# A decoder step's MLP with a third result buffer, finishing work spread over steps, and six row operands kept in high and low parts

## The chip, the core and the metric

The kernel runs on one core of one Trainium2 chip. The metric is the device time of one execution in microseconds. The kernel before took 2792.03 us as the median of three runs (2787.6 to 2799.4). The profile is of one further execution.

The engines named below: TensorE (PE, with PEld for its weight loads), VectorE (DVE), ScalarE (ACT), GpSimd (POOL) and SyncE (SP). POOL and SP mostly issue transfers here, each on a queue of its own. Every engine works through its own instructions in the order in which the program emits them, and waits where an operand is not there yet.

## What is computed

One step of a one-layer decoder for 576 rows (512 of a prompt, 64 of eight samples), all in float32. Cut to what matters here:

```python
D_MODEL = 2048; D_FF = 4 * D_MODEL

x = x + jnp.concatenate([attn, conv_y], axis=-1) @ w_out
hid = jnp.square(jax.nn.relu(rms_norm(x, g_mlp) @ w_up))
x = x + hid @ w_down
gate = jax.nn.sigmoid(rms_norm(x, g_ple) @ w_ple_gate)
x = x + (pe @ w_ple) * gate
y = rms_norm(x, g_final)
```

Ahead of that stand the input projections, attention over a prompt and over a paged cache, and a convolution. The change does not touch them.

## The kernel before

**Phases.** The first phase (up to 860 us of the profile) holds projections, attention and convolution. Then comes the out-projection, 16 output tiles from `outproj` (L1155), up to 1069 us. The second phase (`phase2`, L1300) is the MLP: `up` (group g=1, 32 passes), `down` (g=2, 8 output pairs over 32 operands, cut into rounds), and the gate (g=3, 8 passes), to 2756 us; a final norm and the stores follow.

**Products.** Operands lie transposed, features on the 128 partitions and rows on the free axis. `up` and `down` work on blocks of two by two (a pair of feature tiles, two halves of HR = 288 rows) with seven products instead of eight. Seven sums of weight blocks meet seven sums of row blocks. Each operand is split for TensorE's float32r form into a high part (rounded, an ACT copy) and a low part (the rest, a DVE subtraction), and a product is three matmuls: high by high, high by low, low by high. One *step* is one weight quad against one row operand: 7 products, 21 matmuls of 128 x 288, lines L1460 to L1462. Steps are numbered from 0 at the start of `up`: 256 of `up` (8 per pass), 256 of `down`, then 64 of the gate, whose products are plain.

**A pass's end.** The seven products lie in seven of eight PSUM tiles. `combine_head` (L1543) and `combine_tail` (L1557) add them into a result pair `c` of [128, 2, 576], one of two buffers. The next pass's products need these PSUM tiles: the first has the eighth, the second waits for the ACT copy L1550, the third for L1551, and so on. A pass's *finish* (`fin_up`, `fin_down`, `fin_gate`, `fin_out` for the out-projection) then makes from `c` what the next group needs. `fin_up` scales by the norm (L1314), applies relu and square (L1316, L1317), makes the row sums `T` (`tsums`, L1513) and stores them with `c` to DRAM (`stored`, L1277) as seven blocks in float32, 1008 KB for an operand.

**Row operands.** A ring of eight places holds row operands with high and low parts, [128, 2, 7, 288] each. When a place's last use is past, a hook calls `mk` (L1364): it loads the next stored operand, 1008 KB, into the low half (L1376, on POOL's queue) and queues a *build* (`slot`, L1534): two ACT copies make the high part, two DVE subtractions (864 and 1152 columns) turn the loaded sums into the low part. For the first `up` pass operands 0, 1 and 7 are made in place by `fin_out`, 2 to 6 are loaded once the first phase's operands are off TensorE. At the last `up` pass, steps 248 to 255, the eight places change to `down`'s operands 0 to 7, one per step. `down`'s first round is short: passes of 3, 3, 3, 4, 5, 6, 7 and 8 steps.

**Weights.** `QStream` (L1620) loads two quads at a time on SP's queue (512 KB into one of four `w2r` buffers), sums blocks on DVE (L1648 to L1650) and splits one quad per step into `w2h` (ACT) and `w2l` (DVE), three buffers each, two steps ahead (`prep(t + 2)`).

**Order.** The program writes out each engine's order by hand. `Beside` (L1574) holds two queues of generators, 0 for finishes and 1 for builds. Within each step `run` gives the step's time as credit (2.79 us) and takes pieces from queue 0 first, then 1, while credit lasts. A piece yields its DVE cost; a negative yield -k makes its generator rest for k steps. `EL` (L95) estimates the costs. `flush` emits a generator to its end at once, as when a step needs an operand whose build is not out yet, or at a pass's end, where queue 0 is emptied. The finish of the last `up` pass goes to queue 1.

```python
self.credit = min(max(self.credit, -3.0) + dt, dt)
while self.credit > 0:
    ready = [q[0] for q in self.q if q and q[0][1] <= t]
```

Of the kernel before, what the change touches and what calls it, by code (L numbers as in the profile page):

```python
# [30 lines left out]
DOWN_PART = 7  # L31
RING = 8
OUT_ORDER = (0, 1, 4, 5, 6, 7, 2, 3)

# [108 lines left out]
class Kern:  # L143
# [52 lines left out]
    def build(self):  # L196
        tc, nc, a = self.tc, self.nc, self.a
        with ExitStack() as top:
# [956 lines left out]
    def outproj(self, gen):  # L1155

        nc, a = self.nc, self.a
        self.open2()
        bg, t2 = self.bg, self.t2
        for n in range(KT):  # L1160
            self.on = n
            if n % 2 == 0:
                bg.flush_all(0)
                self.oc_ = t2.tile([128, 2, NR], F32, name="c", tag="c", bufs=2)
            self.rx = t2.tile([128, NR], F32, name="rx", tag="rx", bufs=1)
            nc.sync.dma_start(self.rx, a["x"][:, n, :])
# [12 lines left out]
            gen = self.gemm_tile(self.out_evac)  # L1179
# [36 lines left out]
    def plan(self):  # L1216
# [9 lines left out]
        wsrc = (None, a["w_up"], a["w_down"], a["w_gate"])  # L1226
        loads = []
        for g, p, k0, k1 in segs:
            for k in range(k0, k1, 2):
                m = min(2, k1 - k)  # L1230
                loads.append((wsrc[g][p][:, k:k + m], m, g == 3))
        self.segs = segs
        self.W = QStream(self, loads, EL)
# [10 lines left out]
    def squares(self, p, x):  # L1244

        nc, acc = self.nc, self.acc2
        sq = self.buf("sq2")
        nc.scalar.activation(sq, x, AF.Square)
        yield 0
        if p == 0:  # L1250
            nc.vector.tensor_tensor(acc, sq[:, 0, :], sq[:, 1, :], ALU.add)
            yield EL(NR)
        else:
            for i in range(2):
                nc.vector.tensor_tensor(acc, acc, sq[:, i, :], ALU.add)
                yield EL(NR)
# [8 lines left out]
    def operands(self, c, g):  # L1265

        if g is not None:
# [3 lines left out]
            c = cg  # L1271
            yield 0
# [4 lines left out]
    def stored(self, c, T, dst):  # L1277
        nc = self.nc
        nc.gpsimd.dma_start(dst[:, 0, :], c[:, 0, :HR])
        nc.gpsimd.dma_start(dst[:, 1:3, :].rearrange("p a n -> p (a n)"), c[:, 1, :])  # L1280
        nc.gpsimd.dma_start(dst[:, 3:, :], T)

    def fin_out(self, p, c):
# [10 lines left out]
        else:  # L1294
            self.stored(cg, T, self.up_in[p])
        if p == 7:
            yield from self.squares(p, c)
            self.bg.add(0, self.norm(self.P_))

    def phase2(self):  # L1300
# [12 lines left out]
        def fin_up(p, c, r, final):  # L1313
# [3 lines left out]
            nc.scalar.activation(c, c, AF.Square)  # L1317
            yield 0
            c, T = yield from self.operands(c, None)
            self.stored(c, T, self.down_in[p])  # L1320

# [42 lines left out]
        def mk(g, j):  # L1364
# [9 lines left out]
            def load():  # L1374
                bg.flush(fin_of[g - 1, j])
                nc.gpsimd.dma_start(f(h.lo), src)  # L1376

            if g < 3:
                load()

            def build():
# [14 lines left out]

        quadlist = [(si, k) for si, sg in enumerate(segs) for k in range(sg[2], sg[3])]
        lastuse, seg0 = {}, {}
# [30 lines left out]
        slots[1, 7].work = fin_of[0, 7]  # L1429
        prev = before = behind = None  # L1430
        for t, (si, k) in enumerate(quadlist):
            g, p, k0, k1 = segs[si]
            if prev:
# [16 lines left out]
            hi, lo = W.hl.pop(t)  # L1450
            if k == k0:
                pr = {}
            if g == 3:
                self.plain(pr, hi, lo, s, k == k0, k == k1 - 1)
            else:
                for (i, ia, ib) in self.PRODS:
                    if k == k0:
                        pr[i] = self.P_()
                    o = pr[i][:, :HR]
                    nc.tensor.matmul(o, hi[:, ia, :], s.hi[:, ib, :], start=(k == k0), stop=False)  # L1460
                    nc.tensor.matmul(o, hi[:, ia, :], s.lo[:, ib, :], start=False, stop=False)  # L1461
                    nc.tensor.matmul(o, lo[:, ia, :], s.hi[:, ib, :], start=False, stop=(k == k1 - 1))  # L1462
# [7 lines left out]
            if g == 1 and p == 0 and 2 <= k + 2 < 7:  # L1470
                bg.flush(slots[1, k + 2].work)
            if k == k1 - 1:
                if g != 1 or p:
                    bg.flush_all(0)
                if slow:
                    r = pre[g](p, lastseg[g, p] == si)
                if before:
                    bg.flush(before)
                if g == 3:
                    c = t2.tile([128, 2, NR], F32, name="c", tag="c", bufs=2)  # L1480
                else:
# [61 lines left out]
    def combine_head(self, pr):  # L1543

        nc, t2 = self.nc, self.t2
        q = lambda i: pr[i][:, :HR]
        c = t2.tile([128, 2, NR], F32, name="c", tag="c", bufs=2)
        c11, c12, c22 = c[:, 0, :HR], c[:, 0, HR:], c[:, 1, HR:]
# [25 lines left out]
class Beside:  # L1574


    def __init__(self):
        self.q = [deque(), deque()]
        self.credit, self.now = 0.0, 0
# [21 lines left out]
    def run(self, t, dt):  # L1601
# [18 lines left out]
class QStream:  # L1620
# [15 lines left out]
    def sums(self, l):  # L1636
# [6 lines left out]
        if self.loads[l][2]:  # L1643
# [127 lines left out]
```

## Time and profile before

| | us |
|---|---|
| median of three runs | 2792.03 |
| profiled execution | 2789.04 |
| its span | 2787.3 |
| PE busy | 2702.0 (97%) |
| DVE busy | 2058.4 (74%) |
| ACT busy | 1174.4 (42%) |
| POOL busy | 503.5 (18%) |

The span runs from the first to the last instruction; the execution's time adds what lies around it. Matmuls are pipelined, so PE's busy time overstates its work: where PE lost time is read from the number of matmuls in a stretch instead. A window row gives start and end, length, busy time and instruction count (x) for each engine, the granted TensorE clock (1.00 is full), the DMA engines' busy share, and GB/s. A group or timeline row names line, engine, operation, output and input tile, and in brackets the idle time before it and what ended that. Tiles named `xs` are row operands in the ring, `c` is a result pair, `t` or `wt` a helper of the combination, `ui` and `di` the stored operands of `up` and `down`, `x` the residual in DRAM.

### The profile page before, as it was taken

Reading aid. Unit: us, or ns where it says so; the run is one execution under the profiler, and the core shown is the slowest. Engines: PE = TensorE matmul, PEld = TensorE weight load, DVE = VectorE, ACT = ScalarE, POOL = GpSimd, SP = SyncE. Lnnn points to the kernel's source line nnn. Section 1 sums busy time; section 2 is a strip of 40 time slices with the busy share of each in tenths; the row PEclk is TensorE's granted clock in tenths of the full one; section 3 lists DMA queues with packets and bytes.
Section 4 is the critical chain, followed back from the end, with each engine's and each line's share of the span. In section 5 each row is a group of like instructions: output and inputs, shape, how many; then the busy total and the mean of one; then the engine's idle time right before and its main releaser. Section 6 shows DMA issues by size and latency. Waiting matters only on the chain.

```text
span 2787.3 us, 56961 instructions
## 1 busy us (share of the span) xinstructions
PE 2702.0 (97%) x22201; PEld 2605.8 (93%) x22201; DVE 2058.4 (74%) x3613; ACT 1174.4 (42%) x1755; POOL 503.5 (18%) x896
## 2 busy tenths in 40 slices
PE   8999999999999999999999999989999999999996
PEld 8988889998888998999999999989999999999995
DVE  5677777766654437888888888898888888888444
ACT  4232334345643324444444444544444444444332
POOL 1177766731100000000000000100000000000000
PEclk9999999999999999999999999999999999999998
DMA  4688888888745445444444444655665556555444
GB/s 151 204 286 274 288 284 290 292 299 303 261 141 193 150 154 201 135 149 140 142 142 137 141 138 136 240 148 165 173 177 158 166 170 173 170 175 192 155 157 167
DMA packets 232432, 530.81 MB, mean 190 GB/s; under 512 B 25217, under 2 KB 25858, under 8 KB 232162
## 3 DMA queue, kind: packets, MB, share of 16 engines
q1 hardware_dynamic: 167234, 329.72, 36.7%
q0 software_dynamic: 32096, 137.67, 15.6%
q10 hardware_dynamic: 32832, 59.78, 6.9%
q8 instruction: 174, 2.85, 0.4%
q14 instruction: 96, 0.79, 0.1%
HBM read 431.53 MB, written 95.55 MB: 189 GB/s over the span
## 4 chain that ended last, share of the span: by engine, by line
PE 61%; issue 5%; DVE 4%; ACT 1%; DMA 1%; POOL 0%; DVEq 0%; ACTq 0%; SPq 0%; POOLq 0%
PE P L1461 15%; PE P L1460 15%; PE P L1462 15%; PE U L478 7%; PE P L1503 2%; PE P L1505 2%; PE P L1504 2%; PE U L1109 1%; DVE w2l L152 1%; DVE xs L152 1%; DMA xs<-x 0%; DMA xs<-ui 0%; DVE y L1491 0%; DVE w2r L1648 0%; DMA w2r<-in_w_up 0%
## 5 line engine op out<-in xcount | busy, mean ns | idle before, releaser
L1460 PE MATMUL P<-xs,w2h 128*128 128x288 f32 x3584 | 1066.1, 297 | 20.7 <-DVE c L1551 9.6
L1461 PE MATMUL P<-xs,w2h 128*128 128x288 f32 x3584 | 1065.3, 297 | 4.6 <-DVE xs L152 4.6
L1462 PE MATMUL P<-xs,w2l 128*128 128x288 f32 x3584 | 1061.4, 296 | 3.1 <-DVE w2l L152 3.1
L149 ACT ACTIVATE w2h<-w2r 128x896 fp32r<-128x896 f32 (+1 forms) x576 | 523.4, 915 | 772.2 <-PE P L1461 462.1
L152 DVE TENSOR_TENSOR w2l<-w2r,w2h 128x896 fp32r<-128x896 f32 (+1 forms) x576 | 600.5, 1043 | 208.0 <-ACT w2h L149 207.3
L1460 PEld LDWEIGHTS P<-xs,w2h 128*128 128x128 f32 x3584 | 678.1, 189 | 27.4 <-DVE c L1551 12.5
L1461 PEld LDWEIGHTS P<-xs,w2h 128*128 128x128 f32 x3584 | 678.6, 189 | 6.8 <-DVE xs L152 6.5
L1462 PEld LDWEIGHTS P<-xs,w2l 128*128 128x128 f32 x3584 | 676.5, 189 | 3.8 <-DVE w2l L152 3.8
L478 PE MATMUL U<-xh,whi 128*128 128x288 f32 x1792 | 401.5, 306 | 2.7 <-ACT whi L123 1.4
L478 PE MATMUL U<-xh,wlo 128*128 128x288 f32 x1792 | 385.0, 296 | 2.5 <-DVE wlo L129 2.5
L478 PE MATMUL U<-xl,whi 128*128 128x288 f32 x1792 | 383.9, 296 | 2.0 <-DVE xl L311 2.0
L478 PEld LDWEIGHTS U<-xh,whi 128*128 128x128 f32 x1792 | 288.1, 189 | 23.5 <-issue 16.9
L478 PEld LDWEIGHTS U<-xh,wlo 128*128 128x128 f32 x1792 | 288.5, 189 | 3.7 <-DVE wlo L129 3.7
L478 PEld LDWEIGHTS U<-xl,whi 128*128 128x128 f32 x1792 | 288.5, 189 | 3.2 <-DVE xl L311 3.2
L123 ACT ACTIVATE whi<-wraw 128x512 fp32r<-128x512 f32 x224 | 141.2, 630 | 284.6 <-PE U L478 153.5
L129 DVE TENSOR_TENSOR wlo<-wraw,whi 128x512 fp32r<-128x512 f32 x224 | 159.7, 713 | 102.5 <-ACT whi L123 100.3
L1019 DVE SCALAR_TENSOR_TENSOR y<-ue,cv,y 128x512 f32<-128x512 f32 x240 | 183.3, 764 | 4.2
L1648 DVE TENSOR_TENSOR w2r<-w2r 128x512 f32<-128x512 f32 (+1 forms) x272 | 177.7, 653 | 10.2 <-DMA w2r<-in_w_up 5.1
L1020 POOL TENSOR_SCALAR cvt<-us,cv 128x64 f32<-128x64 f32 x240 | 168.6, 702 | 21.8
L1503 PE MATMUL P<-xs,w2h 128*128 128x288 f32 x512 | 152.2, 297 | 0.1
L1504 PE MATMUL P<-xs,w2h 128*128 128x288 f32 x512 | 151.4, 296 | 0.0
L1505 PE MATMUL P<-xs,w2l 128*128 128x288 f32 x512 | 151.4, 296 | 0.0
(347 smaller groups left out, 2947.7 us busy)
## 6 DMA issues: line engine op xcount, KB each, us to landing
k<-in_cache_kv SPq DMA_DIRECT2D x256, 256.0 KB, 5.0
v<-in_cache_kv SPq DMA_DIRECT2D x256, 256.0 KB, 5.0
w2r<-in_w_up SPq DMA_DIRECT2D x128, 512.0 KB, 4.0
w2r<-in_w_down SPq DMA_DIRECT2D x112, 512.0 KB, 4.3
wraw<-in_w_main ACTq DMA_DIRECT2D x156, 256.0 KB, 5.1
xs<-di POOLq DMA_DIRECT2D x32, 1008.0 KB, 6.1
x<-c POOLq DMA_DIRECT2D x48, 576.0 KB, 7.3
di<-T POOLq DMA_DIRECT2D x32, 576.0 KB, 3.6
```

What stands on the lines that cost most here:

```text
L149: self.nc.scalar.activation(out, in_, AF.Copy, **kw)
L152: self.nc.vector.tensor_tensor(out, in_, f(hi), ALU.subtract)
L478: self.nc.tensor.matmul(u[:, r, :HR], w, x[:, r * HR:(r + 1) * HR], start=first and n == 0, stop=last and n == 2)
L1019: nc.vector.scalar_tensor_tensor(y, ue[:, j:j + NPR], w, y, ALU.mult, ALU.add)
L1020: nc.gpsimd.tensor_scalar(t, us[:, :, j:j + 8], w, None, ALU.mult)
L1460: nc.tensor.matmul(o, hi[:, ia, :], s.hi[:, ib, :], start=(k == k0), stop=False)
L1461: nc.tensor.matmul(o, hi[:, ia, :], s.lo[:, ib, :], start=False, stop=False)
L1462: nc.tensor.matmul(o, lo[:, ia, :], s.hi[:, ib, :], start=False, stop=(k == k1 - 1))
L1503: nc.tensor.matmul(o, hi[:, ia, :], s.hi[:, kh, rows], start=first and kh == 0, stop=False)
L1504: nc.tensor.matmul(o, hi[:, ia, :], s.lo[:, kh, rows], start=False, stop=False)
L1505: nc.tensor.matmul(o, lo[:, ia, :], s.hi[:, kh, rows], start=False, stop=last and kh == 1)
L1648: lambda: V(w[:, :, 4:6, :], w[:, :, 0:1, :].broadcast_to([128, m, 2, 128]), w[:, :, 1:3, :], ALU.add),
```

## The change

Six operands, the pairs in `SPLIT` (group, number), are stored in DRAM already split, [128, 2, 7, 288] of float32r. `stored` makes each part where the sums are: four pieces (288 columns and three of 576), each an ACT copy, a rest of one step, a DVE subtraction, two POOL transfers and another rest. For the `down` operands all four pieces use one buffer `hl`. `mk` loads such an operand whole, 2016 KB, into its place and queues no build.

Result pairs have three buffers instead of two, and a finish must be out only before its buffer is needed again, three passes later, while `up` runs. In a pass's last step `wait` books credit and emits nothing; the combination follows at once. ACT pieces in the finishes now end with a rest of one step (`yield -1`) where they had none. The last `up` finish has a third queue, one piece per step in the passes 1 and 2 of `down`'s rounds. The norm after the out-projection, with the last squares, is a finish of its own. The first `up` pass takes its operands in the order 0, 1, 7, 2, 3, 4, 5, 6. The first weight loads are issued three output tiles earlier, and their block sums are made two tiles earlier (`ahead`). The tile `rx` shares the place of the combination's helper.

```diff
+SPLIT = ((1, 3), (1, 5), (2, 0), (2, 1), (2, 3), (2, 4))
...
+            self.both = {x: dram.tile([128, 2, 7, HR], F32R, name="hl%d_%d" % x) for x in SPLIT}
...
-                self.oc_ = t2.tile([128, 2, NR], F32, name="c", tag="c", bufs=2)
-            self.rx = t2.tile([128, NR], F32, name="rx", tag="rx", bufs=1)
+                self.oc_ = t2.tile([128, 2, NR], F32, name="c", tag="c", bufs=3)
+            self.rx = self.w2.tile([128, NR], F32, name="rx", tag="t5", bufs=1)
...
-                if n == KT - 1 and h == 0:
+                if n == KT - 4 and h == 0:
                     for i in range(4):
                         self.W.dma(i)
+                if n == KT - 3 and h % 2:
+                    bg.spend(self.W.ahead(h // 2))
...
+            if (g, p) == (1, 0):
+                parts = [(0, 2), (7, 1), (2, 2), (4, 2), (6, 1)]
...
         nc.scalar.activation(sq, x, AF.Square)
-        yield 0
+        yield -1
...
+        if x in self.both:
+            T = T.rearrange("p a n -> p (a n)")
+            dst = self.both[x].rearrange("p i a n -> p i (a n)")
+            if x[0] == 2:
+                t = self.t2.tile([128, 2, NR], F32R, name="hl", tag="b", bufs=2)
+                parts = [(t[:, 0, :], t[:, 1, :])] * 4
+            else:
+                parts = [(self.w2.tile([128, 7, 128], F32R, name="hh", tag="w2h", bufs=3).rearrange("p a n -> p (a n)"),
+                          self.w2.tile([128, 7, 128], F32R, name="ll", tag="w2l", bufs=3).rearrange("p a n -> p (a n)"))
+                         for _ in range(4)]
+            o = 0
+            for (hi, lo), y in zip(parts, (c[:, 0, :HR], c[:, 1, :], T[:, :NR], T[:, NR:])):
+                n = y.shape[-1]
+                self.split_hi(hi[:, :n], y)
+                yield -1
+                self.split_lo(lo[:, :n], y, hi[:, :n])
+                for i, part in enumerate((hi, lo)):
+                    nc.gpsimd.dma_start(dst[:, i, o:o + n], part[:, :n])
+                yield EL(n)
+                yield -1
+                o += n
+            return
...
         if p == 7:
-            yield from self.squares(p, c)
-            self.bg.add(0, self.norm(self.P_))
+            self.bg.add(0, self.fin_rows(c))
+
+    def fin_rows(self, c):
+        yield from self.squares(7, c)
+        yield from self.norm(self.P_)
...
             def load():
                 bg.flush(fin_of[g - 1, j])
-                nc.gpsimd.dma_start(f(h.lo), src)
+                if (g, j) in self.both:
+                    nc.gpsimd.dma_start(t, self.both[g, j])
+                else:
+                    nc.gpsimd.dma_start(f(h.lo), src)
 
             if g < 3:
                 load()
+            if (g, j) in self.both:
+                return
...
-                fin_of[pg, pp_] = bg.add(int(late), fins[pg](pp_, c, r, pfinal), 2 if late else None)
-                before, behind = behind, fin_of[pg, pp_]
+                fin_of[pg, pp_] = bg.add(2 if late else 0, fins[pg](pp_, c, r, pfinal))
+                recent.append(fin_of[pg, pp_])
...
-            slow = k0 == 0 and p == 0 and g != 2
-            if k == k1 - 2 and not slow:
-                bg.flush_all(0)
+            if g == 2 and p in (1, 2):
+                bg.nudge(2)
+            slow = p == 0 and g != 2
+            if i == n - 2 and not slow:
+                if g > 1:
+                    bg.flush_all(0)
                 r = pre[g](p, lastseg[g, p] == si)
-            bg.run(1000 + t, 3.18 if g == 3 else 2.79)
...
+            if i == n - 1:
+                bg.wait(1000 + t, 3.18 if g == 3 else 2.79)
+            else:
+                bg.run(1000 + t, 3.18 if g == 3 else 2.79)
...
-                if g != 1 or p:
+                if g > 1:
                     bg.flush_all(0)
...
-                if before:
-                    bg.flush(before)
+                if recent[0]:
+                    bg.flush(recent[0])
...
-            ready = [q[0] for q in self.q if q and q[0][1] <= t]
+            ready = [q[0] for q in self.q[:2] if q and q[0][1] <= t]
...
+    def nudge(self, n):
+
+        if self.q[n]:
+            self.step(self.q[n][0])
+
+    def wait(self, t, dt):
+        self.now = t
+        self.credit = min(max(self.credit, -3.0) + dt, dt)
...
+    def ahead(self, l):
+
+        cost = self.sums(l)
+        self.some(3)
+        return cost
```

More of the change, by code (lines that the diff above doesn't have):

```diff
@@ L1227, in plan @@
         loads = []
+        self.orders = []
         for g, p, k0, k1 in segs:
-            for k in range(k0, k1, 2):
-                m = min(2, k1 - k)
+            parts = [(k, min(2, k1 - k)) for k in range(k0, k1, 2)]
+            if (g, p) == (1, 0):
+                parts = [(0, 2), (7, 1), (2, 2), (4, 2), (6, 1)]
+            for k, m in parts:
                 loads.append((wsrc[g][p][:, k:k + m], m, g == 3))
+            self.orders.append([k + i for k, m in parts for i in range(m)])
         self.segs = segs
@@ L1275, in operands, with stored @@
         return c, T
-    def stored(self, c, T, dst):
+    def stored(self, c, T, x):
         nc = self.nc
+        if x in self.both:
[17 more added lines that the diff above has]
+                yield EL(n)
+                yield -1
+                o += n
+            return
+        dst = (self.up_in, self.down_in)[x[0] - 1][x[1]]
         nc.gpsimd.dma_start(dst[:, 0, :], c[:, 0, :HR])
@@ L1294, in fin_out @@
         else:
-            self.stored(cg, T, self.up_in[p])
+            yield from self.stored(cg, T, (1, p))
         if p == 7:
-            yield from self.squares(p, c)
-            self.bg.add(0, self.norm(self.P_))
+            self.bg.add(0, self.fin_rows(c))
+    def fin_rows(self, c):
+        yield from self.squares(7, c)
+        yield from self.norm(self.P_)
     def phase2(self):
@@ L1317, in fin_up @@
             nc.scalar.activation(c, c, AF.Square)
-            yield 0
+            yield -1
             c, T = yield from self.operands(c, None)
-            self.stored(c, T, self.down_in[p])
+            yield from self.stored(c, T, (2, p))
         def fin_down(p, c, r, final):
@@ L1395, in mk @@
             h.work = bg.add(1, build())
-        quadlist = [(si, k) for si, sg in enumerate(segs) for k in range(sg[2], sg[3])]
+        quadlist = [(si, k) for si, ks in enumerate(self.orders) for k in ks]
         lastuse, seg0 = {}, {}
@@ L1429, in phase2 @@
         slots[1, 7].work = fin_of[0, 7]
-        prev = before = behind = None
+        prev, recent = None, deque([None] * 3, 3)
         for t, (si, k) in enumerate(quadlist):
-            g, p, k0, k1 = segs[si]
+            g, p, *_ = segs[si]
+            ks = self.orders[si]
+            n, i = len(ks), t - seg0[si]
             if prev:
@@ L1476, in phase2 @@
                     r = pre[g](p, lastseg[g, p] == si)
-                if before:
-                    bg.flush(before)
+                if recent[0]:
+                    bg.flush(recent[0])
                 if g == 3:
-                    c = t2.tile([128, 2, NR], F32, name="c", tag="c", bufs=2)
+                    c = t2.tile([128, 2, NR], F32, name="c", tag="c", bufs=3)
                 else:
@@ L1546, in combine_head @@
         q = lambda i: pr[i][:, :HR]
-        c = t2.tile([128, 2, NR], F32, name="c", tag="c", bufs=2)
+        c = t2.tile([128, 2, NR], F32, name="c", tag="c", bufs=3)
         c11, c12, c22 = c[:, 0, :HR], c[:, 0, HR:], c[:, 1, HR:]
@@ L1577, in __init__ @@
     def __init__(self):
[L1578 removed]
+        self.q = [deque(), deque(), deque()]
         self.credit, self.now = 0.0, 0
```

23 lines of the change are left out of this document (11 added, 12 removed).

## The prediction

> **What bounds the kernel now.** I read the page first (span, engines, chain), then busy time by stretches, PE's waits, and the timeline.
>
> ```profile
> span 2787.3 us, 56961 instructions
> PE 61%; issue 5%; DVE 4%; ACT 1%; DMA 1%; POOL 0%; DVEq 0%; ACTq 0%; SPq 0%; POOLq 0%
> core 0: us, PE busy (x) PEld busy (x) DVE busy (x) ACT busy (x) POOL busy (x), PEclk, DMA share, GB/s
> 900.00:1050.00 150.00, 148.50 (x1112) 148.04 (x1111) 60.73 (x90) 45.36 (x67) 11.39 (x21) 1.00 0.50 158
> 1066.00:1146.00 80.00, 69.71 (x488) 66.38 (x489) 69.47 (x111) 40.89 (x48) 6.41 (x12) 0.98 0.49 169
> 1200.00:1780.00 580.00, 580.00 (x4352) 580.00 (x4351) 496.17 (x776) 270.81 (x311) 41.96 (x78) 1.00 0.43 141
> 1780.00:1876.00 96.00, 85.61 (x596) 82.92 (x595) 87.05 (x139) 49.79 (x61) 11.98 (x19) 0.95 0.70 212
> 2084.00:2090.00 6.00, 4.80 (x34) 4.26 (x33) 5.86 (x10) 2.84 (x5) 0.00 (x0) 1.00 0.30 87
> 2243.00:2249.00 6.00, 4.63 (x33) 4.09 (x32) 5.86 (x10) 2.68 (x5) 0.12 (x1) 1.00 0.28 87
> 2400.00:2411.00 11.00, 8.40 (x49) 7.83 (x49) 10.59 (x17) 3.15 (x6) 0.85 (x1) 0.84 0.41 85
> 2500.00:2550.00 50.00, 46.85 (x327) 44.93 (x326) 44.09 (x71) 23.60 (x33) 3.20 (x6) 0.97 0.62 193
> 2755.00:2787.00 32.00, 6.22 (x23) 4.14 (x21) 18.38 (x31) 4.80 (x7) 0.00 (x0) 0.58 0.40 160
> ```
>
> TensorE sets the end. In the undisturbed row it does 4352 matmuls in 580 us, 7.50 per us: one step of 21 takes 2.80 us. What a stretch lost is its length less its count divided by 7.50: 14.9 us at the start of the up projection (1066 to 1146), 16.6 where up passes to down (1780 to 1876), 1.5 + 1.6 + 4.5 = 7.6 at the three starts of a round of down, 6.4 where down passes to the gate. That is 45.5 us, and more the change cannot win in the MLP; the tail after 2755 keeps its order.
>
> ```profile
> PE P L1460 <- ACT c L1550: 4.9, 2, 4.6
> PE P L1460 <- DVE c L1551: 5.2, 3, 2.6
> 2084.67 2.32 DVE L152 TENSOR_TENSOR xs<-xs 128x864 fp32r<-128x864 f32 x2
> 2086.91 0.45 DVE L1551 TENSOR_TENSOR c<-c,P 128x288 f32<-128x288 f32 x1
> ```
>
> The columns are total, times and longest. The first is from the stretch 1780 to 1876, the second from 2080 to 2411 with the three round starts: PE waits for the combination that frees its PSUM tiles. The timeline says why at the first round start: two halves of a row operand's low part (2.32 us) stand on DVE ahead of L1551, which frees the tile.
>
> **Waiting instead of running in a pass's last step.** The last step now only books credit, so no build is emitted ahead of the combination; those two instructions of (2,17), (2,24), (2,31) come in the next two steps, and are not needed for a round. The 7.6 us should go; I leave 0.6 for the DVE work that now follows: **7 saved**. If that cover failed, the 2.32 would stand before another combination, at most 7.6 lost again.
>
> **Up to down.** Four of the eight operands come whole, so their builds vanish:
>
> ```profile
> L152 DVE TENSOR_TENSOR xs<-xs 128x1152 fp32r<-128x1152 f32 x7 | 9.5, 1352 | 0.0
> L152 DVE TENSOR_TENSOR xs<-xs 128x864 fp32r<-128x864 f32 x7 | 7.4, 1052 | 0.0
> 1783.40 0.54 POOL L1376 DMA_DIRECT2D xs<-di  x1 [15.47 <-issue]
> 1785.96 0.54 POOL L1376 DMA_DIRECT2D xs<-di  x1 [2.02 <-PE P L1462]
> 1788.76 0.53 POOL L1376 DMA_DIRECT2D xs<-di  x1 [2.27 <-DVE T L1518]
> 1791.56 0.54 POOL L1376 DMA_DIRECT2D xs<-di  x1 [0.65 <-PE P L1462]
> 1792.27 0.96 ACT L149 ACTIVATE w2h<-w2r 128x896 fp32r<-128x896 f32 x1 [2.87 <-PE P L1462]
> 1793.13 1.97 ACT L149 ACTIVATE xs<-xs 128x864 fp32r<-128x864 f32 x2
> DMA to landing us min/median/max: 5.1/10.8/11.8
> L1376 POOL DMA_DIRECT2D xs<-ui x5: 530/530/541, 1069.8 to 1072.0; - x5
> DMA to landing us min/median/max: 7.5/11.4/16.0
> ```
>
> The first two rows (1779.9 to 1872.3) give 2.40 us of DVE per operand, so 9.6 for four. DVE is busy 87.05 of 96 us there, so it is the limit and 9.6 would count. But the loads double. Five loads issued from 1069.8 to 1072.0 landed from 7.5 to 16.0 us after issue, so 1077.3 to 1088.0: 2.7 us per 1008 KB, one after another. Loads of the down operands are issued one per step end (1785.96, 1788.76, 1791.56), (2,0) first. Now its first bytes land by 1783.40 + 5.1 = 1788.5. With (2,0) and (2,1) doubled, (2,2) lands near 1788.5 + 2.7 + 5.4 + 2.7 = 1799.3, or 1801 with the weights between.
>
> Its build, though, is emitted early. Queue 1 used to hold (2,0), (2,1), (2,2); by credit and the yield of two steps the first build ran in step 252 (ACT at 1793.13). With the first two gone, (2,2), added in step 250, is ripe in 252 and takes that place. ACT works in order: it stands from 1793 to 1801 with nothing landed, and the w2h of step 255 is behind it. Step 251 ends near 1791.5 (the load at 1791.56 waited for it); three w2h buffers let PE go on through 252 to 254, to about 1799.9. That w2h comes at 1801 + 2.0 + 0.95 = 1804, its w2l a microsecond later: PE loses some 5 us. The same again with (2,5), which moves up to step 256: behind (2,2) lie the stores of pass 30 (2.7), (2,3) and (2,4) (10.8) and itself (2.7), so it lands at 1817 to 1820, while ACT reaches it at 1810. Behind it wait the w2h of 259 and the ACT copy that frees PSUM: 5 to 8 us.
>
> In DVE's terms: 87.05 - 9.6 = 77.4 of work, plus about 7.5 and 8 standing still behind ACT, is 93 of the 96 us; what DVE idles today outside that (9 us, part of it around the one-piece up finish of pass 31, which now goes in single steps) partly remains. Bounds: a gain of 11 if nothing is held, a loss of 12 if both holds add whole to what is lost. I take **3 lost**, as both holds are worked out and the saving is inside them.
>
> **Start of up.** Weight loads start three tiles earlier and their sums run in the out-projection, where DVE has room (2 waits of PE for DVE or ACT, 0.7 and 0.6 us, below): 0.8 saved. The order 0, 1, 7, 2, ... gives each loaded operand one step more, but 7 x 1008 KB come instead of 5: the last lands at 1088.0 + 5.4 = 1093.4; its build (a first ACT half of 1.1 and 2.4 on DVE) and its step of 2.8 end pass 0 near 1099.7 at the earliest; now pass 1 begins at 1101.42 (row below, 168 products after the first): 1.7 saved. Later passes: the two 128x896 waits go with the spread finish (2.5 + 1.0).
>
> ```profile
> 1101.42 0.29 PE L1460 MATMUL P<-xs,w2h 128*128 128x288 f32 x1
> PE P L1461 <- DVE xs L152: 3.2, 6, 0.7
> PE P L1462 <- DVE w2l L152: 2.5, 2, 1.6
> PE P L1460 <- DVE c L1551: 1.0, 1, 1.0
> PE U L478 <- DVE wlo L129: 0.7, 1, 0.7
> PE P L1460 <- DVE c L1153: 0.6, 1, 0.6
> L149 ACT ACTIVATE w2h<-w2r 128x896 fp32r<-128x896 f32 x207 | 194.1, 950 | 256.7 <-PE P L1461 189.8 <-PE P L1462 66.9
> L152 DVE TENSOR_TENSOR w2l<-w2r,w2h 128x896 fp32r<-128x896 f32 x208 | 226.0, 1087 | 47.3 <-ACT w2h L149 47.3
> L1518 DVE TENSOR_TENSOR T<-c 128x576 f32<-128x576 f32 x26 | 19.7, 758 | 28.5 <-ACT c L1317 28.5
> di<-T POOLq DMA_DIRECT2D x26, 576.0 KB, 3.6
> di<-c POOLq DMA_DIRECT2D x26, 288.0 KB, 3.4
> x<-c POOLq DMA_DIRECT2D x31, 576.0 KB, 8.5
> ```
>
> Against it stands the making of the parts, in passes 1 to 6 for operands 0, 1, 3, 4: one low part of 288 and three of 576 columns, 0.46 + 3 x 0.76 = 2.7 us of DVE (rows L1518 and L1551; 22.4 - 22.4 x 496.17/580 = 3.2 are free in a pass). One tile serves all four parts, so the next high part on ACT waits until the store before has landed: 0.7 (high) + 0.95 (w2h, behind it) + 1.09 (w2l) + 0.76 (low) + 3.4 (288 KB store) = 6.9 us per turn, and the code gives it two steps, 5.6. Three turns slip 4 us against about as much lead of the weights: 0 to 2 us of PE for each of four operands. I take 3. Sum here: 0.8 + 1.7 + 3.5 - 3 = **3 saved** (bounds: 8 saved, 5 lost). Third result buffer, moved rx and the two stored out-projection operands: nothing, DVE is busy 60.73 of 150 us beside that projection (row 900 to 1050); without that cover 2.7 us each.
>
> **Down to gate.** The new yield after the square lets queue 1 run a step earlier, so the gate operands' builds move up while their loads do not:
>
> ```profile
> 2506.39 1.45 ACT L149 ACTIVATE xs<-xs,vecs 128x576 fp32r<-128x576 f32 x2 [2.32 <-DMA xs<-x]
> ```
>
> ACT waited 2.32 us here already; one step earlier it waits 5. Bounds 0 and 2.8 for each of two such builds ahead of a busy DVE; I take **2 lost**.
>
> **Sum.** 7 - 3 + 3 - 2 = 5 us saved. The profiled execution took 2789.0 (span 2787.3 and 1.7 around it); its runs' median is 2792.0, 3 above. So 2784 on the profiled scale and **2787** as a median.
>
> **Rivals.** *The whole loads come in time* (faster). For it: DVE's 87.05 of 96 is the limit, the holds rest on my landing times. Then up to down gains 11, up's start 8, the rounds 7, and the gate loses nothing: 26, so 2766. It needs (2,2) landed before about 1797 and (2,5) before 1811.
>
> *The new transfers convert* (slower). Source and target are now both F32R, where the old load viewed its target as F32. No transfer of before does that; the nearest row is the copy that does arithmetic on the way, 8.5 us for 576 KB against 3.6 for a plain one. [...] If such a transfer takes as long as the arithmetic one (a factor of 2.4), each whole load takes 13 us instead of 5.4, (2,2) lands 15 us later and (2,5) 30 later in all, and pass 0 ends 15 later: 45 lost, besides 4.8 more per turn of the stores. With half that excess: 22 for the loads, and for the twelve turns 12 x 2.4 = 29 less a lead of some 14, so 22 + 15 - 5 = 32 lost: 2824. Per unit of the factor this is about 52, so from 1.1 on the change is slower than before, and from 1.4 on by over 0.5%. Against it: the arithmetic copy reads two operands, a conversion one.
>
> *The parts do not shorten anything* (the change does not do what it says): holds at both ends of up eat 9.6 + 3.5, the rounds' 7 stay: within the forecast's case.
>
> **Chances.** 0.5% is 14 us, about what runs of this kernel can tell from no change. Forecast case (2779 to 2797) 0.43, loads in time 0.24, converting 0.33. So faster 0.24, same 0.43, slower 0.33. The range 2766 to 2832 leaves out about 0.2, mostly converting loads at the full factor; the forecast's own range is 2779 to 2797.
>
> **What would show it.** PE's wait on DVE L1551 at round starts gone; ACT standing on (2,2)'s and (2,5)'s first build for 5 us or more "<-DMA", with PE's gaps at steps 255 and 259; landing of whole loads near twice that of halves (plain) or four to five times (converting); ACT waiting for stores between high parts in passes 1 to 6. Wrong if up to down loses under 10 us, or if PE stands still in passes 2 to 6 for more than 8.

## The result and the profile after

The changed kernel took 2805.93 us as the median of six runs (2797.77 to 2815.45), the kernel before 2789.69 on the same chip (2780.05 to 2799.4, six runs): a ratio of 1.0058, interval 1.004 to 1.0075. It is slower by 16 us. The profiled execution, of 2797.77 us, is the quickest of the six. Its page has:

```profile
span 2796.0 us, 57025 instructions
PE 29%; DVE 2%; issue 1%; DMA 1%; ACT 0%; DVEq 0%; POOL 0%; ACTq 0%; POOLq 0%
```

The second line is the chain of waits, which could be followed through a third of the span here; TensorE leads it as before. To see where it stood, count steps. A step of up or down is 21 matmuls on L1502 to L1504, which stand for L1460 to L1462 of before. Its length is the distance of two starts on PE's timeline. What it takes over 2.80 us is its loss, summed over the steps longer than 2.84. Ahead of step 0 one matmul of the out-projection serves as a mark, since every kernel waits there for the same weights. Mark and start of step 0 on PE's timeline, after and then before:

```profile
916.89 0.53 PE L480 MATMUL U<-xh,whi 128*128 128x288 f32 x2 [0.96 <-ACT whi L124]
975.78 0.61 PE L480 MATMUL U<-xh,wlo 128*128 128x288 f32 x1 [3.22 <-DVE wlo L130]
1034.76 0.61 PE L480 MATMUL U<-xh,whi 128*128 128x288 f32 x1 [5.95 <-ACT whi L124]
1081.41 0.29 PE L1502 MATMUL P<-xs,w2h 128*128 128x288 f32 x1
```

```profile
920.20 0.40 PE L478 MATMUL U<-xh,whi 128*128 128x288 f32 x1 [0.81 <-ACT whi L123]
1069.39 0.29 PE L1460 MATMUL P<-xs,w2h 128*128 128x288 f32 x1
```

From the mark to step 0 it is 149.2 us before and 164.5 after: 15.3 us are lost in the out-projection, with two waits of 3.22 and 5.95 that the old kernel does not have. The table gives this and the losses by stretch, in us, for the kernels of the study too; no step from 80 to 247 is late in any of them. Each ratio is against the kernel before on the same chip.

| kernel | mark to step 0 | steps 0 to 79 | 248 to 279 | 280 to 489 | 490 to 510 | median | ratio (interval) |
|---|---|---|---|---|---|---|---|
| before | 149.2 | 16.3 | 16.9 | 8.8 | 6.5 | 2789.7 | 1 |
| after | 164.5 | 18.5 | 21.1 | 2.9 | 10.8 | 2805.9 | 1.0058 (1.004 to 1.0075) |
| parts_none | 148.2 | 10.0 | 15.1 | 2.5 | 11.3 | 2775.7 | 0.9944 (0.9925 to 0.9963) |
| parts_down | 148.2 | 23.7 | 20.2 | 1.2 | 10.5 | 2790.3 | 1.0007 (0.9991 to 1.0022) |
| parts_up | 161.2 | 10.8 | 13.7 | 2.2 | 11.7 | 2788.4 | 0.9999 (0.9984 to 1.0013) |
| three_pairs | 151.8 | 20.3 | 20.9 | 2.3 | 10.0 | 2793.0 | 1.0012 (0.9999 to 1.0025) |
| pairs_later | 151.7 | 20.8 | 9.7 | 1.3 | 10.2 | 2781.7 | 0.9976 (0.9965 to 0.9987) |
| none_square | 148.2 | 10.3 | 14.0 | 1.9 | 5.5 | 2776.5 | 0.9943 (0.9921 to 0.9966) |
| none_empty | 148.2 | 19.1 | 13.0 | 1.2 | 11.9 | 2783.5 | 0.9979 (0.9967 to 0.9991) |
| none_run | 148.2 | 12.9 | 17.6 | 7.3 | 19.3 | 2797.1 | 1.0026 (1.0013 to 1.0038) |
| weights_late | 161.9 | 22.5 | 20.6 | 1.6 | 11.1 | 2807.2 | 1.0068 (1.0053 to 1.0083) |
| best_short | 148.2 | 36.0 | 10.2 | 0.9 | 5.6 | 2795.7 | 1.0031 (1.002 to 1.0043) |
| best_two | 148.3 | 18.0 | 10.9 | 2.4 | 5.2 | 2779.1 | 0.9972 (0.996 to 0.9983) |
| none_two_buffers | 148.2 | 10.0 | 14.7 | 2.0 | 12.3 | 2772.8 | 0.9941 (0.9924 to 0.9957) |

After against before: 15.3 + 2.2 + 4.2 - 5.9 + 4.3 = 20.1 us. The two profiled executions differ by only 8.7. Of the rest, 3.3 us lie ahead of the mark (916.89 against 920.20), and about 8 come from a quicker pace of PE that this execution happened to have (last section).

**The out-projection.** The changed kernel's timeline at the second stored operand, ScalarE's and the transfers' rows:

```profile
1023.66 2.70 SPq L1690 DMA_DIRECT2D w2r<-in_w_up  x4
1025.65 1.01 ACT L150 ACTIVATE hh<-cg 128x288 fp32r<-128x288 f32 x2
1026.37 0.53 POOL L1305 DMA_DIRECT2D hl<-hh  x1 [2.33 <-ACT hh L150]
1027.38 0.69 ACT L150 ACTIVATE hh<-T 128x576 fp32r<-128x576 f32 x1 [0.72 <-DVE T L1568]
1033.50 0.68 ACT L150 ACTIVATE hh<-T 128x576 fp32r<-128x576 f32 x1 [5.44 <-DMA hl<-hh]
1034.09 0.61 ACT L124 ACTIVATE whi<-wraw 128x512 fp32r<-128x512 f32 x1
```

Three high parts are made one after another. The fourth needs the tile of the first, whose store was issued at 1026.37. ScalarE stands 5.44 us for it, and the cast of the projection's own weights (L124), for which TensorE waits, stands behind. The clock then falls too; the stretch from 1034 to 1041, in the columns of the prediction's windows (the clock is the figure third from the end):

```profile
1034.00:1041.00 7.00, 6.24 (x33) 6.16 (x34) 3.30 (x5) 2.60 (x5) 1.06 (x2) 0.67 1.09 361
```

The granted clock is 0.67 there, behind a wait of 5.95 us, against 1.00 in the row 900 to 1050 of before. From 1030 to 1034, where TensorE runs no matmul, it is 0.72, and from 1041 to 1045 it is 1.00 again.

**Up to down.** ScalarE's first build of (2,2), its load and TensorE's wait behind it, from the timeline, then the first build of (2,5):

```profile
1796.91 0.53 POOL L1414 DMA_DIRECT2D xs<-di  x1 [2.23 <-PE P L1504]
1800.39 0.96 ACT L150 ACTIVATE w2h<-w2r 128x896 fp32r<-128x896 f32 x1 [2.69 <-PE P L1504]
1809.38 1.98 ACT L150 ACTIVATE xs<-xs 128x864 fp32r<-128x864 f32 x2 [8.03 <-DMA xs<-di]
1812.25 0.61 PE L1502 MATMUL P<-xs,w2h 128*128 128x288 f32 x1 [4.57 <-ACT w2h L150]
1826.57 0.93 ACT L150 ACTIVATE xs<-xs 128x864 fp32r<-128x864 f32 x1 [6.71 <-DMA xs<-di]
```

ScalarE stands 8.03 and 6.71 us. The matmul at 1812.25 opens step 255. The loads themselves, in the page's list of transfers (KB each, median us to landing), and the DMA traffic while the whole loads run (last two figures: share and GB/s):

```profile
xs<-di POOLq DMA_DIRECT2D x28, 1008.0 KB, 6.1
xs<-hl POOLq DMA_DIRECT2D x6, 2016.0 KB, 14.0
1798.00:1812.00 14.00, 9.68 (x74) 9.44 (x72) 6.84 (x11) 3.58 (x4) 3.21 (x6) 0.93 1.02 386
```

At 386 GB/s, if most of it is theirs, a load of 2016 KB (2.06 MB) takes 5.3 us: twice the 2.7 of a 1008 KB load, not four or five times. The first two whole loads, (2,0) and (2,1), show it directly, with their times from issue to landing:

```profile
L1412 POOL DMA_DIRECT2D xs<-hl x1: 541/541/541, 1791.6 to 1791.6; - x1
DMA to landing us min/median/max: 7.9/7.9/7.9
L1412 POOL DMA_DIRECT2D xs<-hl x1: 532/532/532, 1794.1 to 1794.1; - x1
DMA to landing us min/median/max: 10.9/10.9/10.9
```

They landed at 1799.5 and 1805.0, 5.5 us apart, about what two loads of 1008 KB took before the change (5.4). A conversion that costs time does not show in this trace.

**Rounds and gate.** The three round starts, with 34, 33 and 49 matmuls before, and ScalarE's first builds of two gate operands:

```profile
2094.00:2100.00 6.00, 6.00 (x48) 6.00 (x47) 5.83 (x12) 4.20 (x5) 0.85 (x1) 1.00 0.31 87
2250.50:2256.50 6.00, 6.00 (x47) 6.00 (x46) 5.86 (x11) 4.15 (x5) 0.88 (x1) 1.00 0.48 102
2408.00:2419.00 11.00, 10.53 (x78) 10.17 (x77) 10.83 (x19) 5.69 (x6) 0.84 (x1) 1.00 0.57 111
```

```profile
2511.46 0.78 ACT L150 ACTIVATE xs<-xs,vecs 128x576 fp32r<-128x576 f32 x1 [4.62 <-DMA xs<-x]
2529.14 0.78 ACT L150 ACTIVATE xs<-xs,vecs 128x576 fp32r<-128x576 f32 x1 [3.41 <-DMA xs<-x]
```

At the rounds TensorE hardly stands any more: by 7.50 matmuls per us, 0.6 us are missing at the third. At the gate ScalarE waits 4.62 and 3.41 us, where it waited 2.32 and not at all.

### The profile page after: what moved, and what is told of

Read it like the earlier page. It is cut to its first block, busy times and chain, and to the rows that moved or that the text cites. A ratio compares the mean times of both kernels' runs of the same rounds, so it can differ in the third digit from the quotient of the medians.

```text
span 2796.0 us, 57025 instructions
## 1 busy us (share of the span) xinstructions
PE 2703.4 (97%) x22201; PEld 2603.6 (93%) x22201; DVE 2056.0 (74%) x3628; ACT 1175.0 (42%) x1767; POOL 516.5 (18%) x926
## 5 line engine op out<-in xcount | busy, mean ns | idle before, releaser
L1502 PE MATMUL P<-xs,w2h 128*128 128x288 f32 x3584 | 1067.7, 298 | 21.5 <-DVE c L1599 9.7
L1504 PE MATMUL P<-xs,w2l 128*128 128x288 f32 x3584 | 1058.1, 295 | 4.8 <-DVE w2l L153 4.7
L1502 PEld LDWEIGHTS P<-xs,w2h 128*128 128x128 f32 x3584 | 677.2, 189 | 29.7 <-DVE c L1599 13.6
L1504 PEld LDWEIGHTS P<-xs,w2l 128*128 128x128 f32 x3584 | 678.8, 189 | 8.3 <-DVE w2l L153 8.1
L124 ACT ACTIVATE whi<-wraw 128x512 fp32r<-128x512 f32 x224 | 141.1, 630 | 286.6 <-PE U L480 155.9
```

Source lines behind the costliest of these rows:

```text
L1502: nc.tensor.matmul(o, hi[:, ia, :], s.hi[:, ib, :], start=(i == 0), stop=False)
```

## The experiments

**First: which operands cost it.** Three kernels differ from the changed one in the list alone, and a fourth in the tiles.

```diff
-SPLIT = ((1, 3), (1, 5), (2, 0), (2, 1), (2, 3), (2, 4))
+SPLIT = ()                                    # parts_none
+SPLIT = ((2, 0), (2, 1), (2, 3), (2, 4))      # parts_down
+SPLIT = ((1, 3), (1, 5))                      # parts_up
```

> All steps of the change but no operand in parts. Counting what steps lost over 2.80 us and the start of the first step, the change cost 12.0 us ahead of step 0 (two gaps of PE in the out-projection, 3.4 and 6.1 us), 2.1 at the start of up, 4.3 at up to down, 4.3 at down to gate, and saved 6.0 at the rounds. Theory (the parts cost ahead of step 0 and at up to down; the steps earn the rounds): step 0 starts within 1.5 us of 1069.4, steps 248 to 280 lose 15 to 18 as before the change, the rounds stay saved, the gate's loss stays at 9 to 12: about 3 us below the kernel before, 2784 to 2790. Rival (the moved weight loads and steps cost, the parts do not): step 0 stays near 1081, and the time near 2804.

> Only the four operands of down in parts. Theory: no gap in the out-projection, step 0 near 1069; steps 248 to 280 lose 20 to 23, with ACT standing 6 to 8 us on each of the builds of (2,2) and (2,5); about the kernel before plus 1, 2788 to 2794. Rival (the parts of up delay down too, or the hold at (2,2) comes from elsewhere): steps 248 to 280 lose 15 to 18.

> Only the two operands of up in parts. Theory: the gaps in the out-projection stay (step 0 near 1081), steps 248 to 280 lose 15 to 18 and ACT stands less than 3 us there; the turns of the one tile in passes 1 to 6 go and with them the 2.3 us at steps 24 and 48: about 2796 to 2802. Rival: if the 12 us came from the stores of down or from noise, step 0 lies near 1069 and the time near 2788.

The parts_none ratio is 0.9944: all the rest of the change is a gain, of 12.5 us by the medians and of some 15 by the ratio. That is more than the 2784 to 2790 us expected, as the start of up gains too (16.3 to 10.0). Adding the operands of down costs 0.63% (0.9944 to 1.0007), adding those of up 0.55%. The two together would make 1.0062, and the changed kernel stands at 1.0058: within these intervals nothing else is needed. In the steps 0 to 79 the two do touch each other, since parts_down loses 23.7 there and the changed kernel 18.5. By the table the parts of up cost 13 us between mark and step 0 (148.2 to 161.2). The parts of down cost 5 at steps 248 to 279 and, which I had not looked for, 13.7 in steps 0 to 79. parts_up came out quicker than the 2796 to 2802 expected: without the parts of down the start of up loses 7.7 less than in the changed kernel, where I had put 2.3.

> As the change, but the first two parts of an out-projection operand (288 and 576 columns) share one tile of 896, so that four parts take three pairs of tiles and no part waits for the store of another part of its own operand. Theory (ring): ACT's waits of 5.4 and 0.5 us on the store of a high part and DVE's of 4.9 and 2.8 go, the gaps of 3.4 and 6.1 us on PE become under 1.5 each, step 0 starts at 1070 to 1073, and the time falls by 8 to 11, to about 2796. Rival (the work itself, 4 high and 4 low parts between the weights' casts): the gaps stay, the time stays within 3 of the changed kernel. Rival (the moved weight loads hold the stores): the first gap goes, the second stays over 3.

```diff
-                         for _ in range(4)]
+                         for _ in range(3)]
+                a, b = parts[0]
+                parts = [(a[:, :HR], b[:, :HR]), (a[:, HR:], b[:, HR:])] + parts[1:]
```

The mark now lies 151.8 us ahead of step 0, 12.7 less, and the ratio falls from 1.0058 to 1.0012. The same eight casts and subtractions and the same stores are made as in the changed kernel. TensorE's waits from 960 to 1045 (total, times, longest) in this kernel:

```profile
PE U L480 <- DVE wlo L130: 1.7, 2, 0.9
PE U L480 <- ACT whi L124: 0.8, 2, 0.4
```

These are all of TensorE's waits there, and neither ScalarE nor DVE waits for a store any more. The same length of the out-projection in the changed kernel and in three_pairs:

```profile
957.00:1042.00 85.00, 74.88 (x529) 74.08 (x528) 33.08 (x50) 25.61 (x39) 11.64 (x22) 0.92 0.60 189
960.00:1045.00 85.00, 82.47 (x613) 81.53 (x612) 39.94 (x64) 27.30 (x42) 11.67 (x22) 1.00 0.63 202
```

In 85 us there are 84 matmuls more, which is 11.2 us at 7.50 per us, and the granted clock is full again (1.00 against 0.92): the slow clock went with the waits. The work alone costs 151.8 - 148.2 = 3.6 us. The ring of three tiles made the stall.

**The moved weight loads.** The last kernel on this stretch puts them back where they were.

> The changed kernel (2805.9), with the first weight loads and their sums of the up projection back in the last tile of the out-projection, where they were before the change; the parts stay. The second store of a high part took 7.1 us to land and the gap behind it was 6.1 us, against 3.4 at the first operand; four loads of 512 KB stand just ahead of the second. Theory (the moved loads lengthen the second wait): the gap near 1034 falls from 6.1 to 3 to 4 us, the first stays at 3.4, and step 0 starts about 2 to 3 us earlier less what the later weights cost there (0.6 to 2). Rival (the store lands late by itself, behind the 576 KB store of x on its own queue): both gaps stay, at 3.4 and 6.1.

```diff
-                if n == KT - 4 and h == 0:
+                if n == KT - 1 and h == 0:
...
-                if n == KT - 3 and h % 2:
-                    bg.spend(self.W.ahead(h // 2))
```

The second gap on PE falls from 6.1 to 3.4 us and the first stays at 3.4; step 0 comes 2.6 us sooner after the mark. So the four loads at 1023.66 do lengthen the second wait, but the time did not fall: the start of up lost 4.0 more.

**Why making the parts of down is dear.** This kernel has no operand in parts, but keeps the steps that making them took.

> As parts_none, but the finish of (2,0), (2,1), (2,3), (2,4) has eight empty steps of one step each after its stores, as many as the making of the parts has; no work, no extra transfer. Making those parts raised the loss of steps 8 to 80 from 4.8 to 18.5 us. Theory (steps: a finish that lasts eight steps longer pushes the finishes behind it up to the end of a pass, where they are forced ahead of the combination): steps 8 to 80 lose 10 or more, and the time rises by 5 to 10 to 2781 to 2786. Rival (work: 2.7 us of DVE and 3 of ACT per operand, and the turns of the one tile): steps 8 to 80 lose 4 to 6 and the time stays within 3 of 2775.7.

```diff
         nc.gpsimd.dma_start(dst[:, 3:, :], T)
+        if x in ((2, 0), (2, 1), (2, 3), (2, 4)):
+            for _ in range(8):
+                yield -1
```

Steps 0 to 79 lose 19.1 us instead of 10.0, and the median rises by 8 us, with no work added. DVE's timeline at the end of a pass in this kernel, the rows that matter, and TensorE's wait from 1180 to 1270:

```profile
1185.27 0.75 DVE L1569 TENSOR_TENSOR T<-c 128x576 f32<-128x576 f32 x1
1186.06 0.46 DVE L1571 TENSOR_TENSOR T<-c,T 128x288 f32<-128x288 f32 x1
1186.55 0.46 DVE L1572 TENSOR_TENSOR T<-T,c 128x288 f32<-128x288 f32 x1
1186.92 1.35 DVE L1352 TENSOR_TENSOR c<-c,rb 128x1152 f32<-128x1152 f32 x1
...
1189.53 0.45 DVE L1602 TENSOR_TENSOR c<-c,P 128x288 f32<-128x288 f32 x1
```

```profile
PE P L1505 <- DVE c L1602: 6.3, 2, 3.2
```

The sums T of one operand and the scaling c by rb of the next stand ahead of the combination (L1602, which is L1599 of the changed kernel). A finish that is eight steps longer fills a pass of eight steps. Those behind it slip until the end of a pass forces them, all before the combination. What the change took away at the rounds it makes anew here. The late steps are 40 and 64 (3.9 and 4.4 us), and parts_down has its own at the same two (4.7 and 6.1). In the changed kernel the sums T stand ahead of L1599 at steps 24 and 48 instead, and cost less (2.25 and 2.24).

**The build ahead of its load.** The builds of (2,2) and (2,5) are let come later, on top of three_pairs; (2,2) is used in step 258 and (2,5) in step 279.

> As three_pairs (2793.0), but the builds of (2,2) and (2,5) become ripe 5 and 8 steps after they are added instead of 2. Theory (ACT held by builds that are put ahead of their loads eats the 9.6 us of DVE that the four whole loads save): ACT's waits of 8.0 and 6.7 us on these loads go to under 2 each, steps 248 to 280 lose 8 to 13 instead of 20.9, under the 15.1 without parts, and the time falls by 8 to 12, to 2781 to 2785. Rival (the loads' transfers or DVE bound this stretch whatever the order): steps 248 to 280 lose 18 or more, with PE waiting for DVE in other places, and the time stays at 2790 or more.

```diff
-                yield -3 if g == 2 and j >= RING else -2
+                yield {2: -5, 5: -8}.get(j, -2) if g == 2 and j < RING else -3 if g == 2 else -2
```

Steps 248 to 279 lose 9.7 us instead of 20.9, and the ratio falls from 1.0012 to 0.9976. ScalarE's timeline at the build of (2,2):

```profile
1807.01 0.95 ACT L150 ACTIVATE w2h<-w2r 128x896 fp32r<-128x896 f32 x1 [0.69 <-PE P L1505]
1807.87 0.91 ACT L150 ACTIVATE xs<-xs 128x864 fp32r<-128x864 f32 x1
```

The build follows the weights without a wait, and the loss is 5.4 less than without parts (15.1). So the DVE work that the four whole loads save seems to show only now; before, ScalarE's standing ate it. No run lets builds come later without parts; but in parts_none ScalarE does not wait for these loads at all, so there is no such wait to win there.

**The last step and the square.** Two single lines of parts_none are put back as they were before the change.

> As parts_none, with run in a pass's last step as before the change. Theory (builds ahead of the combination): the three round starts lose 5 to 8 again instead of 0.9 for the three, PE waits for L1599 there by 2 to 3 us, and the time rises by 5 to 8, to 2781 to 2784. Rival (the third result buffer alone took the stall away): the round starts lose under 2, and the time stays within 2 of 2775.7.

> As parts_none (2775.7), with yield 0 instead of yield -1 after the square, as before the change. Theory (the wait after the square lets a gate operand's build be put ahead of its load, so that ACT stands): ACT's waits on the loads of x fall from 8 us in two to about 2.3 in one, steps 490 to 511 lose 6 to 7 instead of 11.3, and the time falls by 3 to 5, to 2771 to 2773. Rival (the third result buffer or the wait in the last step costs this): steps 490 to 511 lose 10 to 12 and the time stays at 2773 to 2778.

```diff
-                bg.wait(1000 + t, 3.18 if g == 3 else 2.79)
+                bg.run(1000 + t, 3.18 if g == 3 else 2.79)     # none_run
...
-        yield -1
+        yield 0      # none_square, after the activation Square
```

With run, the three round starts lose 6.6 us again (1.74, 1.58 and 3.28; 0.9 in all without it), but the time rises by 21 (2775.7 to 2797.1). The largest further loss is at the gate, 8 us, most of it one wait of TensorE; its waits from 2075 to 2415 and from 2485 to 2560 in this kernel:

```profile
PE P L1502 <- DVE c L1599: 4.7, 3, 2.7
PE P L1502 <- ACT c L1598: 7.5, 1, 7.5
```

Neither theory had that size. ScalarE's rows ahead of that wait show the same kind of hold:

```profile
2544.29 1.44 ACT L150 ACTIVATE xs<-xs,vecs 128x576 fp32r<-128x576 f32 x2 [6.43 <-DMA xs<-x]
2545.64 0.39 ACT L1598 ACTIVATE c<-P 128x288 f32<-128x288 f32 x1
```

A gate operand's build, emitted in the pass's last step, stands 6.43 us for its load, and the copy that frees the PSUM tile is behind it. With the square as before, ScalarE's waits for the gate's loads (2485 to 2560) fall; first none_square, then parts_none:

```profile
ACT xs L150 <- DMA xs<-x: 3.5, 2, 2.0
ACT xs L150 <- DMA xs<-x: 12.5, 3, 5.2
```

The stretch loses 5.5 instead of 11.3, as expected, but the medians do not part (0.9943 and 0.9944, each within 0.2%). The loss has moved: two steps inside the gate, 517 and 518, take 12.0 us instead of 7.2. The same 53 matmuls, first none_square, then parts_none:

```profile
2552.90:2565.00 12.10, 9.63 (x53) 8.36 (x52) 6.49 (x11) 4.41 (x7) 0.00 (x0) 0.86 0.32 106
2557.80:2565.10 7.30, 7.30 (x53) 6.82 (x52) 5.84 (x12) 3.08 (x5) 0.00 (x0) 1.00 0.44 117
```

From step 490 to the last matmul of the gate it is 275.6 us before the change, 280.5 in parts_none and 279.2 in none_square. The yield after the square thus explains most of ScalarE's waits, but only about 1.3 of the 4.9 us that parts_none loses there against the kernel before; what makes the others stays open.

**Is there a better version?** Two kernels keep parts of down alone, with the square as before and the builds let come later; best_short drops the step between high and low part, best_two keeps only (2,0) and (2,3).

> parts_down with yield 0 after the square, the builds of (2,2) and (2,5) ripe 5 and 8 steps after they are added, and no step between the high and the low part (four steps shorter in a finish). Theory: steps 248 to 280 lose 8 to 12 (no hold), 490 to 511 lose 5 to 7, steps 8 to 80 lose 6 to 11 instead of 18.5 (half of the extra steps); sum of the losses 22 to 32 against 39 in parts_none and 31.7 in none_square, time 2766 to 2776. Rival (the tile's turn now stops ACT for each store): steps 8 to 80 lose 15 or more, time 2778 or above.

> Only (2,0) and (2,3) in parts, yield 0 after the square, builds of (2,1) and (2,4) ripe 4 and 7 steps after they are added. Theory (a finish eight steps longer can be made up for in the two short passes behind it): steps 8 to 80 lose 5 to 9, steps 248 to 280 lose 10 to 13 (4.8 us less DVE work than without parts), 490 to 511 lose 5 to 7: 2768 to 2776, at or just below parts_none. Rival (every long finish costs its 3 us by itself, whatever follows): steps 8 to 80 lose 10 or more and the time is 2777 or above.

```diff
                 self.split_hi(hi[:, :n], y)
-                yield -1      # best_short
...
+SPLIT = ((2, 0), (2, 3))      # best_two
+                yield {1: -4, 4: -7}.get(j, -2) if g == 2 and j < RING else -3 if g == 2 else -2
```

best_short is a miss: steps 0 to 79 lose 36.0 us. ScalarE's wait from 1090 to 1300:

```profile
ACT hl L150 <- DMA hl<-hl: 20.1, 6, 4.4
```

Without that step the next high part comes before the store has landed, and ScalarE, which also casts the weights, stands for it. best_two loses 18.0 there, 8 more than without parts, for 3 to 4 saved at 248 to 279: 2779.1. Both rivals held. Parts pay in no form tried here. Both kernels also have the long step 517 of none_square (6.49 us).

> As parts_none (2775.7), with two result buffers instead of three, and a finish forced at the end of the pass after its own instead of one pass later. Theory (the third buffer gives the finishes, which wait in a pass's last step, the room to end late): steps 8 to 80 lose 8 to 15 instead of 4.8, the stretch 490 to 511 a little more, and the time rises by 4 to 12, to 2780 to 2788. Rival (waiting in the last step earns all of it, two buffers are enough): the losses stay within 2 in each stretch and the time within 3 of 2775.7.

```diff
-                self.oc_ = t2.tile([128, 2, NR], F32, name="c", tag="c", bufs=3)
+                self.oc_ = t2.tile([128, 2, NR], F32, name="c", tag="c", bufs=2)
...
-        prev, recent = None, deque([None] * 3, 3)
+        prev, recent = None, deque([None] * 2, 2)
```

The tile c is given two buffers in all three places. No stretch moves by more than 1.0 and the ratio stays (0.9941). Without parts the third buffer earns nothing that these runs can tell.

## Why the prediction was wrong

It forecast 5 us saved, and 16 were lost. The step that failed is the one that said of the third buffer, the moved rx "and the two stored out-projection operands: nothing, DVE is busy 60.73 of 150 us beside that projection". A busy share says whether there is room for the work, and the work did cost only 3.6 us for both operands (three_pairs). It says nothing of waiting: four parts go through three tiles, and the fourth stops ScalarE and DVE until a store has landed (5.44 and 4.87 us at the second operand), with the projection's own weights behind it. That is 12.7 us; with the 3.6 of work, and 1.0 that the rest of the change gains, it makes the 15.3. I had worked out just this turn for the operands of down, where one tile serves all parts, and did not ask it of the other branch of the same function. The clause "without that cover 2.7 us each" priced work too, so even the bad case of this term, 5.4 for both, was a third of what it cost. The out-projection has no place among the signs of being wrong either, and neither of the two that were named came: up to down lost over 10, and passes 2 to 6 lost 6.6, under 8. The time lies inside 2766 to 2832 by luck: the slow side of that range was made for converting loads, a term that no run shows: the whole loads landed 5.5 us apart, twice the 2.7 of a 1008 KB load.

Point by point:

- *Rounds, 7 saved:* right, 7.7 at the three round starts (8.6 to 0.9); the column has 5.9, as other steps lose 1.8 more there. Mis-sized beyond it: waiting in the last step is worth 21 us in all without the parts, since running there loses again at the gate, the start of up, and up to down.
- *Up to down, 3 lost:* right, 4.2. The holds are where they were put: steps 254 and 255 lose 8.5 and step 259 loses 4.4, while the two late steps of before, 258 and 262, fall from 13.0 to 5.8. After a start 8.25 us later (step 248 at 1788.15 against 1779.9), (2,2) was to land at 1801 + 8.25 and did at 1809.38; ScalarE's waits were 8.03 and 6.71 us. pairs_later shows them to be the cause.
- *Start of up, 3 saved:* wrong sign, 2.2 lost. The gains of 0.8, 1.7 and 3.5 are 16.3 - 10.0 = 6.3 without the parts, as a sum; no run parts them. The price of the parts, set at 3 for the one tile's turns, is 8.5 here and 13.7 in parts_down. The term's mechanism failed: in parts_down most of it is the length of the finishes in steps (none_empty, 9.1), which I counted only as a slip of the stores. In the changed kernel the two bursts make 4.5 of the 8.5; what makes the rest, and why the price is lower there, stays open.
- *Down to gate, 2 lost:* the waits came as said, and the stretch lost 4.3. But none_square shows that the yield after the square, to which the term put it, accounts for only a small part of what is lost by the end of the gate.
- *Rivals:* the converting transfer was the author's supposition; its price of 13 us a load is refuted by the loads' landings, 5.5 us apart; the loads in time, by the 8.03. The slower outcome came, but by a cause that was not among the rivals.

## What to carry to other kernels

For every tile that a transfer reads, count how many are made before the first comes free, and look at what stands behind the next one on the engine that makes it: a low busy share does not answer this (60.73 of 150 us for DVE here, and 12.7 us lost). Work spread over steps has a length as well as a cost, and a longer chain in a queue that is forced at a deadline returns as a burst just there (9.1 us at steps 0 to 79 in none_empty). And a load made larger shifts every build behind it; let the builds come later by as much, or an engine that works in order stands for them, as ScalarE did for 8.03 and 6.71 us.

## What the runs showed of the hardware

In these traces TensorE has two paces at full granted clock. The stretch 1325 to 1765 has no wait of PE in either kernel, after first and then parts_none:

```profile
1325.00:1765.00 440.00, 440.00 (x3342) 440.00 (x3341) 379.13 (x595) 207.83 (x238) 32.18 (x60) 1.00 0.45 143
1325.00:1765.00 440.00, 440.00 (x3302) 440.00 (x3301) 375.53 (x591) 205.83 (x236) 32.18 (x60) 1.00 0.45 141
```

3342 matmuls against 3302 in the same time, with the same code: a step takes 2.766 or 2.80 us. A pace held for hundreds of steps; in the changed kernel's execution the quick one began after step 69 and ended with step 379, both themselves late (2.94 and 3.30 us). The changed kernel's profiled execution had 327 steps below 2.785, the one before 85, parts_none 24 and none_two_buffers 251. At 0.034 us a step this moves a whole execution by up to 11 us, which is as much as most of the terms above. It is also why the losses by stretch tell these kernels apart better than one time does. What chooses the pace stays open.
